# Regrouping a decoder layer's up projections, down passes and attention stages on one Trainium2 core

## The chip, the core and the metric

The kernel runs on one NeuronCore of a Trainium2 chip. Its engines are TensorE (PE in the profile; PEld is its weight load), VectorE (DVE), ScalarE (ACT), GpSimd (POOL) and SyncE (SP, which here only issues transfers). The metric is the device time of one execution in microseconds, as the median of several runs. A profiled execution additionally yields the span of the core and a trace of every instruction.

## The reference

One decoder layer in float32, for one sequence of 256 tokens and a width of 2048:

```python
h = rmsnorm(x, norm_mix_pre)
xr, yr, q, k, v, g_rnn, g_attn = split(h @ w_in)
y_rnn = rg_lru(causal_depthwise_conv(xr), ...) * gelu(yr)
y_att = sliding_window_sink_attention(rope(q), rope(k), v, sinks)   # 32 query, 4 key heads of 64
mix = sigmoid(g_rnn) * (y_rnn @ w_rnn_proj) + sigmoid(g_attn) * (y_att @ w_attn_proj)
x = x + rmsnorm(mix @ w_out, norm_mix_post)
h = rmsnorm(x, norm_mlp_pre)
u = square(relu(h @ w_mlp_up))                                       # 2048 -> 8192
x = x + rmsnorm(u @ w_mlp_down, norm_mlp_post)                       # 8192 -> 2048
```

The attention window is 128 tokens, worked in blocks of 128: the first block of queries (tb = 0) sees 128 keys, the second (tb = 1) sees 256. The scores are masked, the softmax has one more term per head (the sink), and the probabilities multiply the values.

## The kernel before

**Split products.** A float32 value is split into a high part (rounded to a format that TensorE multiplies at full rate) and a low part (the rest). A product is then high x high + high x low + low x high, three matmuls. Activations are split when they are made; weights are split as they stream in.

**The weight stream.** Class `Stream` (L54 to L156) loads weights as halves of 128 x 1024 float32 (512 KB) on SP's queue into four buffers `wraw` (L76), casts each to its high part `whi` on ScalarE (L94) and subtracts on VectorE for the low part `wlo` (L95). There are six buffers each of `whi` and `wlo`. `ws.half()` hands out the next half and calls `ahead`, which splits up to six halves beyond and loads up to ten beyond; `ws.half(False)` splits no more than it hands out. A buffer of `whi` or `wlo` is written again when TensorE has used it, a `wraw` when both parts are made.

**Two kinds of passes.** In `a_pair` (L243) the weights stand in TensorE's array and the activations stream through, so the result is transposed (channels in partitions). One `a_pair` computes 256 channels for 256 tokens. It takes four halves: f = 0 and 1 are two blocks of 128 channels, and each has two halves of the 2048 inputs. For a half, eight matmuls of 512 columns multiply the high weights with both parts of the activations (they stand side by side), and eight of 256 columns multiply the low weights with the high activations, into the second half of the same bank. At the end ScalarE copies one half of the result and VectorE adds the other (L260, L261). `a_pair` makes the inputs of the convolution and of the gelu (16 pairs), and 30 of the 32 pairs of the up projection; the first two have their own code (`up_pair`). In `b_step` and `b_pass512` the activations stand and the weights stream, always 512 columns wide.

**Work placed between.** A list `waiting` holds generators (`keys_values`, `attention`, `merge`, `residual`). Each call of `pump()` runs the first one to its next `yield`. A pass of the attention gates pumps eight times, a pass of queries four times, and an `a_pair` four times. So a `yield` moves the rest of a generator by one such step in program order. The order of instructions on each engine is then set by a planner before the run: it takes the instructions in program order as their priority, picks for each engine the first that is ready by its own estimate of costs, and gives out buffers as it goes. `pin` keeps instructions in the order written, `high_priority` moves them forward, and `issue_after` puts them behind a named instruction of their queue. On the chip each engine runs its instructions in that order and waits where an input is late.

**Attention.** For a group g of eight heads the stages are rope and transposes of the queries, then `scores` (products on PE, then scale, mask and maximum on VectorE, L543 and L545), `softmax` (maximum with the sink, exponentials on ScalarE at L559, division on VectorE at L564), `turn_probs` (transposes on PE, L581, and copies on ScalarE), and the product with the values (L607). Scores of both blocks were traced ahead of `softmax(0)`. The first norm's `first_norm` (L411) multiplies a diagonal with ones on PE (L425, tile `pr`) to spread the row scale over the partitions as `rT`; the convolution reads it.

**The MLP's beginning.** The second half of the rows of the out projection ends while the first half is already being multiplied with the up weights: `up_step` (L951), 48 products for tb = 0 with high weights, of which 26, 6, 6 and 6 stand ahead of the four transposes `turned(1, q)` of the second block (L958).

**The down projection.** It runs twice (f = 0, 1, each with 4096 of the 8192 inputs) over two passes n of 1024 output columns. The inputs are 16 pairs p of 128-row blocks. Seven of them (`SEVEN`: 0, 2, ... 12) are multiplied as 2 x 2 blocks with seven products instead of eight (`LEFT`): sums of weight blocks (`split_sums`, L114, tiles t, thi, tlo) with sums of activations (tile `seven`). The other nine are plain: two halves, four output blocks, three matmuls each. The last two (14, 15) are held, and done one output block after the other, so that `finish` can begin on the first while others still run. Output blocks lie in eight banks: P1, P6, Q5, N7 in two pairs of banks (tile `s`), which `a_pair` uses too, and P2, Q3, Q4, Cs in four single banks (tiles `dP`, `dQ`, `dCs`). When pair 12 is done, ScalarE and VectorE combine the seven products (L1102 to L1106), and `early` adds what the first half of the MLP had left in DRAM (`acc`). In the last pass two of these four additions ran on GpSimd, and `early` issued the two 1 MB loads of the residual `x1` on ScalarE's queue (L1174). `finish` adds, squares, normalises with the last gain, adds the residual (L1200) and stores.

**Room.** The pool `big` has 12 buffers of 8 KB a partition. uT (the plain pairs' activations) takes five, h2T four in the first half of the MLP, acc two in the second; t, thi and tlo take one each, later g3, `spare` and x1 as well.

## Time and profile before

| | |
|---|---|
| median of three runs | 1519.63 us (1518.05 to 1521.94) |
| profiled execution | 1518.56 us |
| its span | 1516.8 us |
| granted clock of TensorE | 0.997 |
| busy: PE, DVE, ACT, POOL | 99%, 73%, 55%, 0% |
| read from HBM | 288.60 MB, 194 GB/s over the span |

In the profile a row of the groups gives line, engine, operation, output <- inputs, shape and count, then busy time in us and the mean in ns. A row of the waits reads "engine, line <- who released it: us in total, times, longest". A row of the chain gives start, duration, engine, tile and line. A row of a timeline gives start, duration, engine, line, operation and tiles, and in brackets the idle time before it with its releaser. The duration of one matmul (0.39 us) contains its way through the array; the next one starts earlier, so spacing is read from starts. All starts are us from the start of the span.

### The profile page before, as it was taken

Reading aid. Unit: us, or ns where it says so; the run is one execution under the profiler, and the core shown is the slowest. Engines: PE = TensorE matmul, PEld = TensorE weight load, DVE = VectorE, ACT = ScalarE, POOL = GpSimd, SP = SyncE. Lnnn points to the kernel's source line nnn. Section 1 sums busy time; section 2 is a strip of 40 time slices with the busy share of each in tenths; the row PEclk is TensorE's granted clock in tenths of the full one; section 3 lists DMA queues with packets and bytes.
Section 4 is the critical chain, followed back from the end, with each engine's and each line's share of the span. In section 5 each row is a group of like instructions: output and inputs, shape, how many; then the busy total and the mean of one; then the engine's idle time right before and its main releaser. Section 6 shows DMA issues by size and latency. Waiting matters only on the chain.

```text
span 1516.8 us, 20055 instructions
## 1 busy us (share of the span) xinstructions
PE 1496.4 (99%) x7600; PEld 1259.9 (83%) x7600; DVE 1103.0 (73%) x1377; ACT 828.7 (55%) x1143; POOL 5.5 (0%) x11
## 2 busy tenths in 40 slices
PE   9999999999999999999999999999999999999997
PEld 7787778788888888888888888888888888888885
DVE  6666677858769967555657866688886666688897
ACT  6554654747566756443355655555454555555453
POOL 0000000000000000000000000000000000000001
PEclk9999999999999999999999999999999999999998
DMA  6645445455646565555764755566667565566564
GB/s 253 219 143 187 142 131 182 150 186 165 218 157 221 168 208 194 192 183 193 270 220 138 271 192 189 183 189 215 218 200 239 198 189 187 181 236 207 208 212 176
DMA packets 82896, 296.20 MB, mean 195 GB/s; under 512 B 9712, under 2 KB 9968, under 8 KB 81648
## 3 DMA queue, kind: packets, MB, share of 16 engines
q1 hardware_dynamic: 79056, 284.43, 57.3%
q10 hardware_dynamic: 3744, 10.50, 1.9%
q8 instruction: 59, 0.97, 0.3%
q14 instruction: 37, 0.30, 0.1%
HBM read 288.60 MB, written 6.29 MB: 194 GB/s over the span
## 4 chain that ended last, share of the span: by engine, by line
PE 82%; DVE 9%; DMA 5%; ACT 2%; issue 2%; DVEq 0%; SPq 0%; ACTq 0%
PE ps L253 22%; PE ps L256 11%; PE dQ L1061 4%; DMA wraw<-in_w_dn 4%; PE pp L271 4%; PE pp L275 4%; PE pp L273 4%; PE g L271 3%; PE g L275 3%; PE g L273 3%; DVE wlo L95 3%; PE s L1061 2%; PE dP L1061 2%; PE q L273 2%; PE q L275 2%; PE q L271 2%
## 5 line engine op out<-in xcount | busy, mean ns | idle before, releaser
L95 DVE TENSOR_TENSOR wlo<-wraw,whi 128x1024 fp32r<-128x1024 f32 x523 | 635.1, 1223 | 314.0 <-ACT whi L94 313.1
L94 ACT CAST whi<-wraw 128x1024 fp32r<-128x1024 f32 x523 | 544.5, 1052 | 576.6 <-PE ps L253 134.2
L253 PE MATMUL ps<-h2T,whi 128*128 128x512 f32 x960 | 240.5, 393 | 0.0
L253 PEld LDWEIGHTS ps<-h2T,whi 128*128 128x128 f32 x960 | 172.8, 189 | 30.8
L256 PEld LDWEIGHTS ps<-h2T,wlo 128*128 128x128 f32 x960 | 131.0, 191 | 9.3
L256 PE MATMUL ps<-h2T,wlo 128*128 128x256 f32 x960 | 133.9, 283 | 0.0
L253 PE MATMUL ps<-hT,whi 128*128 128x512 f32 x512 | 129.7, 394 | 0.0
L1061 PE MATMUL dQ<-whi,uT 128*128 128x512 f32 x288 | 106.9, 389 | 0.0
L253 PEld LDWEIGHTS ps<-hT,whi 128*128 128x128 f32 x512 | 91.9, 189 | 17.6 <-issue 1.5
L271 PE MATMUL g<-whi,hT 128*128 128x512 f32 x256 | 101.3, 396 | 0.0
L273 PE MATMUL g<-wlo,hT 128*128 128x512 f32 x256 | 100.1, 391 | 0.1
L275 PE MATMUL g<-whi,hT 128*128 128x512 f32 x256 | 99.9, 390 | 0.0
L256 PEld LDWEIGHTS ps<-hT,wlo 128*128 128x128 f32 x512 | 69.9, 190 | 5.0
L256 PE MATMUL ps<-hT,wlo 128*128 128x256 f32 x512 | 71.6, 283 | 0.0
L1061 PEld LDWEIGHTS dQ<-whi,uT 128*128 128x128 f32 x288 | 54.1, 188 | 11.2
L271 PEld LDWEIGHTS g<-whi,hT 128*128 128x128 f32 x256 | 48.1, 188 | 10.5 <-issue 1.0
L1061 PE MATMUL dQ<-wlo,uT 128*128 128x512 f32 x144 | 56.2, 390 | 0.5 <-DVE wlo L95 0.5
L275 PEld LDWEIGHTS g<-whi,hT 128*128 128x128 f32 x256 | 48.1, 188 | 10.1
L273 PEld LDWEIGHTS g<-wlo,hT 128*128 128x128 f32 x256 | 48.2, 188 | 10.0 <-DVE wlo L95 0.5
L1061 PE MATMUL dCs<-whi,uT 128*128 128x512 f32 x144 | 54.1, 389 | 0.0
L1061 PE MATMUL dP<-whi,uT 128*128 128x512 f32 x144 | 54.1, 389 | 0.0
L130 DVE TENSOR_TENSOR tlo<-t,thi 128x1536 fp32r<-128x1536 f32 x28 | 49.2, 1757 | 5.4 <-ACT thi L129 5.3
(280 smaller groups left out, 2464.8 us busy)
## 6 DMA issues: line engine op xcount, KB each, us to landing
wraw<-in_w_up SPq DMA_DIRECT2D x128, 512.0 KB, 4.8
wraw<-in_w_dn SPq DMA_DIRECT2D x128, 512.0 KB, 4.6
wraw<-in_w_g SPq DMA_DIRECT2D x64, 512.0 KB, 4.5
wraw<-in_w_xy SPq DMA_DIRECT2D x64, 512.0 KB, 4.6
wraw<-in_w_q SPq DMA_DIRECT2D x32, 512.0 KB, 4.5
wraw<-in_w_ap SPq DMA_DIRECT2D x32, 512.0 KB, 4.4
wraw<-in_w_rp SPq DMA_DIRECT2D x32, 512.0 KB, 4.3
wraw<-in_w_out SPq DMA_DIRECT2D x32, 512.0 KB, 5.2
```

What stands on the lines that cost most here:

```text
L94: self.pin(self.nc.scalar.copy(hi, src))
L95: self.pin(self.nc.vector.tensor_tensor(lo, src, hi.bitcast(F32), ALU.subtract))
L130: v.tensor_tensor(lo, t, hi.bitcast(F32), ALU.subtract)
L253: mm(both, hi[:, k * P : k * P + P], a.rearrange("p a b -> p (a b)"), start=half == 0 and k == 0, stop=False)
L256: mm(ps[:, f, 1, :], lo[:, k * P : k * P + P], a[:, 0, :], start=False, stop=half == 1 and k == 7)
L271: mm(banks[tb][n], a[:, 0, t], hi[:, n * 512 : n * 512 + 512], start=first, stop=False)
L273: mm(banks[tb][n], a[:, 0, t], lo[:, n * 512 : n * 512 + 512], start=False, stop=False)
L275: mm(banks[tb][n], a[:, 1, t], hi[:, n * 512 : n * 512 + 512], start=False, stop=last)
L1061: mm(b, a[x], w[y], start=not begun and i == 0, stop=tail and i == 2)
```

## The change

- `a_pair` takes its four halves in another order: the high products of halves 0 and 1 and the first one of half 2, then the low products of all four halves, then the other high products of half 2 and those of half 3. The number and widths of the products stay. The calls to `ws.ahead` stand behind the low products of halves 0 and 1 and ahead of the last high group.
- `first_norm` no longer multiplies on PE; `spread_out` does, behind the key transposes of the first block.
- `softmax(0)` is traced ahead of the scores of block 1, and two more `yield`s stand ahead of `turn_probs(0)`.
- 30 instead of 26 up products stand ahead of the first `turned(1, 0)`, and none is left behind the last.
- The passes n = 0 of the down projection run in the order 1, 0, 3, 2, 5, 4, 7, 6, 9, 8, 11, 10, 12, 13, 14, 15; the weight stream is reordered to match. The first (plain) pair runs output block by output block through `step`. The passes n = 1 keep their order.
- In the last pass all four additions of `early` run on VectorE, and the residual is loaded on SP's queue behind the last weight load (`residual_back`).

```diff
+TURNS = ((1, 0, 3, 2, 5, 4, 7, 6, 9, 8, 11, 10, 12, 13, 14, 15), tuple(range(PAIRS)))
...
-            self.nc.sync.dma_start(t, self.chunks[j // 2][:, c])
+            self.load = self.nc.sync.dma_start(t, self.chunks[j // 2][:, c]).ins
...
-            sums.update(len(chunks) + i for i in SEVEN)
-            chunks += [w_dn[(2 * f + n) * PAIRS + i] for i in range(PAIRS)]
+            sums.update(len(chunks) + i for i, p in enumerate(TURNS[n]) if p in SEVEN)
+            chunks += [w_dn[(2 * f + n) * PAIRS + p] for p in TURNS[n]]
...
-        for f in range(2):
-            both = ps[:, f].rearrange("p a b -> p (a b)")
-            for half in range(2):
-                hi, lo = ws.half()
-                act = [acts[kt // 4][:, kt % 4] for kt in range(half * 8, half * 8 + 8)]
-                for k, a in enumerate(act):
-                    mm(both, hi[:, k * P : k * P + P], a.rearrange("p a b -> p (a b)"),
-                       start=half == 0 and k == 0, stop=False)
-                for k, a in enumerate(act):
-                    mm(ps[:, f, 1, :], lo[:, k * P : k * P + P], a[:, 0, :], start=False,
-                       stop=half == 1 and k == 7)
-                pump()
+        def run(j, part, ks=range(8)):
+            f, half = j // 2, j % 2
+            for k in ks:
+                kt = half * 8 + k
+                a, w = acts[kt // 4][:, kt % 4], parts[j][part][:, k * P : k * P + P]
+                if part:
+                    mm(ps[:, f, 1, :], w, a[:, 0, :], start=False, stop=j == 1 and k == 7)
+                else:
+                    mm(ps[:, f].rearrange("p a b -> p (a b)"), w, a.rearrange("p a b -> p (a b)"), start=kt == 0,
+                       stop=j == 3 and k == 7)
+        at = ws.at
+        parts = [ws.half()]
+        run(0, 0)
+        parts.append(ws.half(False))
+        run(1, 0)
+        pump()
+        parts.append(ws.half(False))
+        run(2, 0, (0,))
+        run(0, 1)
+        ws.ahead(at + 1)
+        pump()
+        run(1, 1)
+        ws.ahead(at + 2)
+        run(2, 1)
+        parts.append(ws.half(False))
+        run(3, 1)
+        pump()
+        run(2, 0, range(1, 8))
+        ws.ahead(at + 3)
+        run(3, 0)
+        pump()
...
-            mm(pr[:, tb * P : tb * P + P], ones, dg, start=True, stop=True)
-        nc.scalar.copy(rT, pr[:, 0:S])
+    def spread_out():
+        pr = bank(psm, "pr")
+        for tb in range(TB):
+            mm(pr[:, tb * P : tb * P + P], ones, spread[:, tb * P : tb * P + P], start=True, stop=True)
+        nc.scalar.copy(rT, pr[:, 0:S])
...
+            if tb == 0:
+                spread_out()
             yield
...
         scores(0, 0, [bank(psm, "sc") for par in range(2)])
+        softmax(0)
         scores(1, 0, [bank(psb, "sc") for par in range(2)])
         if not last_group:
             scores(1, 1, two_banks("sc"))
-        softmax(0)
         yield
         if last_group:
             scores(1, 1, [bank(psb, "sc") for par in range(2)])
         softmax(1)
+        yield
+        yield
         yield
         turn_probs(0)
...
-    for q, n in enumerate((26, 6, 6, 6)):
+    for q, n in enumerate((30, 6, 6, 6)):
...
-        for p in range(PAIRS - held):
+        for p in turns[:PAIRS - held]:
...
+            elif p == turns[0]:
+
+                step(p, [ws.half() for i in range(2)], DOWN_ORDER)
...
         parts = [[ws.half(False) for i in range(2)] for p in range(held)]
+        split()
...
-                (nc.gpsimd if n and tb else nc.vector).tensor_tensor(t, t, acc[tb][:, c], ALU.add)
-            if n == 1:
-                for tb in range(TB):
-                    x1.append(flat(unit(f"x1{tb}", F32)))
-                    nc.scalar.dma_start(x1[tb], x1_away[tb])
+                nc.vector.tensor_tensor(t, t, acc[tb][:, c], ALU.add)
+
+        def residual_back():
+
+            for tb in range(TB):
+                x1.append(flat(unit(f"x1{tb}", F32)))
+                with tc.issue_after(ws.load):
+                    ws.load = nc.sync.dma_start(x1[tb], x1_away[tb]).ins
...
-        down(f, n, uT, 2, [(0, 0), (0, 1), (1, 0), (1, 1)], finish, early, between)
+        down(TURNS[n], uT, 2, [(0, 0), (0, 1), (1, 0), (1, 1)], finish, early, between, residual_back)
```

More of the change, by code (lines that the diff above doesn't have):

```diff
@@ L409, in layer @@
     rT = pa.tile([P, S], F32, name="rT")
+    spread = t2("spread")
     def first_norm():
-        pr = bank(psm, "pr")
-        spread = t2("spread")
         for tb in range(TB):
@@ L1067, in layer, with down @@
     PLACE = {(0, 0): "Q4", (0, 1): "Cs", (1, 0): "P2", (1, 1): "Q3"}
-    def down(f, n, uT, held, order, finish, early, between=lambda p: None):
+    DOWN_ORDER = ((1, 1), (1, 0), (0, 0), (0, 1))
+    def down(turns, uT, held, order, finish, early, between=lambda p: None, split=lambda: None):
         two = [pair(f"s{i}") for i in range(2)]
@@ L1150, in layer @@
                 full.clear()
-        order = [(1, 1), (1, 0), (0, 0), (0, 1)]
+        order = DOWN_ORDER
         if f == 0:
@@ L1158, in finish @@
                     nc.scalar.dma_start(acc_away[tb][:, c], t)
-                down(f, n, uT, 2, order, finish, lambda ready: None)
+                down(TURNS[n], uT, 2, order, finish, lambda ready: None)
             continue
@@ L1203, in layer @@
         n = 0
-        down(f, n, uT, 2, order, finish, early)
+        down(TURNS[n], uT, 2, order, finish, early)
         n = 1
```

3 lines of the change are left out of this document (1 added, 2 removed).

## The prediction

> **What bounds the kernel now.** I read the page first (busy shares), then the waits of PE, then the chain that ended last over the whole span, then the timeline of single engines around each wait.
>
> ```profile
> span 1516.8 us, 20055 instructions
> PE 1496.4 (99%) x7600; PEld 1259.9 (83%) x7600; DVE 1103.0 (73%) x1377; ACT 828.7 (55%) x1143; POOL 5.5 (0%) x11
> L253 PE MATMUL ps<-h2T,whi 128*128 128x512 f32 x960 | 240.5, 393 | 0.0
> L253 PE MATMUL ps<-hT,whi 128*128 128x512 f32 x512 | 129.7, 394 | 0.0
> PE pt L581 <- DVE s L564: 3.6, 3, 1.4
> PE pr L425 <- DVE spread L424: 0.9, 1, 0.9
> PE ptr L898 <- DVE h L892: 0.7, 1, 0.7
> PE s L1061 <- DVE u L261: 0.6, 2, 0.3
> PE dQ L1061 <- DVE wlo L95: 0.5, 1, 0.5
> ```
>
> The profiled execution took 1518.56 us, 1.76 us outside its span, and lies 1.07 us under the median of the three runs (1519.63). I sum against the execution and carry the difference to the median.
>
> The reader is to see that TensorE is the bound throughout. The last five rows are waits of PE (us in total, times, longest). Their total is about 6 us, and they are the only large ones. The change removes no matmul, so it can gain only at these waits, at the spacing of the matmuls, and at the end, where other engines finish after PE.
>
> **Part 1, the four halves of `a_pair`.** Before, each half ran eight matmuls 512 wide (high part) and then eight 256 wide (low part), so the width changed eight times in a pair. After, the order is wide, 32 narrow, wide, and the last wide group runs on into the next pair's first: two changes in a pair. The chain of waits gives what a change of width costs:
>
> ```profile
> 827.54 5.76 PE ps L998 x48
> 833.30 1.84 PE ps L995 x8
> 853.31 1.84 PE ps L253 x8
> ...
> 984.59 1.85 PE ps L253 x8
> ...
> 1067.77 2.72 PE dQ L1061 x12
> 1070.49 2.72 PE dP L1061 x12
> ```
>
> In long runs 48 narrow matmuls take 5.76 us (120.0 ns each), and 12 wide ones start 2.72 us before the next twelve (226.7 ns each). Eight wide ones behind narrow ones take 1.84 us, 0.027 more than 8 x 0.2267. From 853.31 to 984.59 lie 47 halves, 2.793 us each; by the rates of long runs a half would be 1.813 + 0.960 = 2.773. So one wide-narrow turn costs 0.020 us. A pair now takes 4 x 2.793 = 11.173 us; after, 32 x 0.2267 + 32 x 0.120 + 0.020 = 11.114. The wide matmuls of this kind are 960 + 512 = 1472, 32 to a pair: 46 pairs. Gain 46 x 0.059 = **2.7 us**. The wide matmuls at 833.30, behind 48 narrow ones, take the same 1.84 as behind eight, so the cost does not grow with the narrow run.
>
> [...]
>
> The other side of this part is the weight buffers. The high halves of the third and fourth quarter are held until about 9.3 and 11.1 us into a pair (7.4 and 10.2 before), and the calls that split ahead come later. A half that takes such a buffer is needed only in the pair after next, 11 us or more later, while its cast and subtraction take 1.05 + 1.22 us. The cover is 8 us; I cost it at nothing. Without that cover each pair would wait up to 2.3 us.
>
> **Part 2, `spread_out`.** The two transposing products of the first norm now come behind the first key transposes.
>
> ```profile
> 43.79 0.39 PE L275 MATMUL g<-whi,hT 128*128 128x512 f32 x1
> 45.10 0.49 PE L425 MATMUL pr<-spread,ones 128*128 128x128 f32 x2 [0.92 <-DVE spread L424]
> ```
>
> PE loses 1.31 - 0.23 = 1.08 us here. The keys' rope and transposes come later than `spread`, so nothing is waited for at the new place; what is left is about 0.1 us of restart. Gain **1.0 us** (0 to 1.1: rT is used only in the convolution, 200 us later).
>
> **Part 3, attention.** `softmax(0)` is traced before `scores(1)`, and the probabilities are turned two stages later.
>
> ```profile
> 151.75 1.28 DVE L543 SCALAR_TENSOR_TENSOR s<-sc,mask 128x512 f32<-128x512 f32 x2
> ...
> 156.51 0.16 DVE L552 TENSOR_TENSOR stat<-stat,sink 128x8 f32<-128x8 f32 x1
> ...
> 161.89 1.29 DVE L564 TENSOR_TENSOR s<-s,stat 128x512 f32<-128x512 f32 x2
> 160.91 0.39 PE L271 MATMUL q<-whi,hT 128*128 128x512 f32 x1
> 162.73 1.23 PE L581 MATMUL pt<-ident,s 128*128 128x128 f32 x8 [1.43 <-DVE s L564]
> ```
>
> PE comes to the transposes of block 0 just after 160.91 and stands 1.59 us beyond its 0.23. VectorE had spent 151.75 to 156.51 on the scores of block 1 before it began the softmax of block 0. With the order turned, that softmax begins up to 4.8 us earlier, its last product ends near 158, and the two extra stages keep PE from coming before the end of the gate pass. Three waits of 3.6 us and 0.16 us of restart each make 4.1. The cover is thinner in the last group, where `scores(1, 1)` waits for its banks and three small VectorE operations (0.2 us each) now stand ahead; between 0 and 4.4 I take **3.6**.
>
> **Part 4, 30 instead of 26 products before the first turn to the MLP.**
>
> ```profile
> 812.90 3.27 PE L954 MATMUL ps<-h2T,whi 128*128 128x256 f32 x26
> 816.91 0.66 PE L898 MATMUL ptr<-ident,h 128*128 128x128 f32 x4 [0.74 <-DVE h L892]
> ```
>
> Four more at 0.12 fill **0.5 us** of that wait; VectorE's normalised row stays late for the rest, and ScalarE and VectorE behind the later turns keep their pace. Bounds 0 and 0.7.
>
> **Part 5, a plain pair opens the passes n = 0.**
>
> ```profile
> 998.80 0.39 PE L1061 MATMUL dQ<-thi,seven 128*128 128x512 f32 x1
> 999.48 0.50 PE L1061 MATMUL s<-thi,seven 128*128 128x512 f32 x1 [0.29 <-DVE u L261]
> 999.82 0.40 PE L1061 MATMUL s<-tlo,seven 128*128 128x512 f32 x1
> ```
>
> The first seven-product pair needs the second `s` pair of banks 3.4 us into the pass, while VectorE still empties it of the last up product (L261). PE loses 0.45 + 0.11 us, in both such passes. The plain pair writes only the four `d` banks, long free, for 24 x 0.227 = 5.45 us. Gain **1.1 us**.
>
> The new order of pairs ends ... 11, 10, 12, 13: two seven-product pairs follow each other, where a plain pair stood between. In the first MLP half, 12 room buffers less 5 for uT and 4 for h2T leave 3, one set of t, thi and tlo. So the second pair's thi can start only when the first pair's products are done:
>
> ```profile
> 1051.94 1.49 ACT L129 CAST thi<-t 128x1536 fp32r<-128x1536 f32 x1 [0.71 <-PE s L1061]
> 1053.46 1.76 DVE L130 TENSOR_TENSOR tlo<-t,thi 128x1536 fp32r<-128x1536 f32 x1 [0.68 <-ACT thi L129]
> 1057.41 0.39 PE L1061 MATMUL s<-whi,seven 128*128 128x512 f32 x1
> 1060.36 0.39 PE L1061 MATMUL dQ<-tlo,seven 128*128 128x512 f32 x1
> ```
>
> Cast and subtraction end 3.28 us after the release. PE asks for tlo 1060.36 - 1057.41 = 2.95 us into a pair; today a plain pair's 5.45 us lie ahead of that. Cost 3.28 - 2.95 + 0.11 = **0.45 us**, once: the second half has two more buffers free (acc's 2 in place of h2T's 4). Bounds: 0, and 3.3 us in each of the two passes if other casts stand ahead of thi.
>
> **Part 6, the end.** The residual's two loads leave ACT's queue at the last seven-product pair and go on SP's behind the last weights; two additions leave POOL for VectorE.
>
> ```profile
> 1483.64 8.09 DMA wraw<-in_w_dn
> wraw<-in_w_dn SPq DMA_DIRECT2D x20, 512.0 KB, 4.5
> x<-x_away ACTq DMA_DIRECT2D x2, 1024.0 KB, 8.7
> 1497.04 0.50 PE L1061 MATMUL dQ<-wlo,uT 128*128 128x512 f32 x1 [0.54 <-DVE wlo L95]
> 1498.82 2.38 DVE L1170 TENSOR_TENSOR t<-t,acc 128x512 f32<-128x512 f32 x2
> 1501.12 0.68 DVE L1187 TENSOR_TENSOR acc<-dQ,t 128x512 f32<-128x512 f32 x1
> 1505.58 0.39 PE L1061 MATMUL dQ<-whi,uT 128*128 128x512 f32 x1
> 1507.89 0.68 DVE L1187 TENSOR_TENSOR acc<-dQ,t 128x512 f32<-128x512 f32 x1
> ```
>
> One of the last weights took 8.09 us to land against a median of 4.5, with 2 MB of residual in flight. Without it the last four come some 3.6 us earlier, and PE's wait of 0.54 (0.7 with its restart) goes. VectorE's additions, now 2.38 us for two, become four of 0.6 each: the same 2.4 us, but done before the first product ends. Then VectorE follows PE instead of trailing it: the last sum starts at 1507.89, some 2.1 us after the last matmul is through; PE done 0.7 earlier and VectorE half a microsecond behind gives about 1505.6. Gain **2.2 us**, between 0.7 (the wait alone) and 2.7. The residual, 2 loads of 8.7 us issued near 1486.5, lands by 1496 to 1504 and is first read near 1502: that cover is thin if the two follow each other at that rate. SP has only output stores queued behind them.
>
> **Sum.** 2.7 + 1.0 + 3.6 + 0.5 + 1.1 - 0.45 + 2.2 = 10.65 us. 1518.56 - 10.65 = 1507.9 for a profiled execution; carried to the median, 1519.63 - 10.65 = **1509.0**.
>
> **The rivals.**
> - *Turns of width are free* and the 0.027 belongs to something else at those places, such as the first use of a new weight half. Against it: in the passes of 512-wide products new halves begin too, and twelves stand at 2.72. The time is 1509.0 + 2.7 = 1511.7. [...]
> - *Attention's waits stay*: the planner moves PE's visits forward with the earlier softmax, and PE again comes before VectorE. For it: today's visits come as early as the planner's costs allow. Against it: the two added stages. 1509.0 + 3.6 = 1512.6.
> - *The residual comes late*: it lands at 1504 rather than before 1502, the output of the first block waits, and the gain at the end is gone: 1511.2.
> - *The two seven-product pairs collide*: 3.3 us exposed in each pass, 6.6 instead of 0.45: 1515.2.
> - *Slower: weights run late in `a_pair`.* Buffers come free in a burst at the end of a pair, and the split for the next wide group arrives after PE. Place: the first wide matmuls of a pair, 46 times. It decides from 10.65/46 = 0.23 us a pair; with 0.5 us it gives 1509.0 + 23 = 1532. Against it are the 8 us of cover counted above and VectorE's 73%.
>
> **How the numbers follow.** Forecast 0.50; free turns 0.12; attention 0.14; residual 0.10; collision 0.07; late weights 0.07. The range reaches from 1505.5 (all upper ends: 2.8 + 1.1 + 4.4 + 0.7 + 1.1 + 2.7 = 12.8, and about a microsecond for small waits that move) to 1516.5, over the collision. About 0.3% (4.6 us, so 1515.1) is what a measurement of this kernel can tell from no change. Faster by more: the first four cases, 0.86. Within 0.3%: the collision, 0.07. Slower: late weights, 0.07.
>
> **What would show it.** In the new profile: pieces of 32 narrow matmuls at 120 ns and pairs at 11.11 us; no wait of `pr`; `pt` waits under 0.5 us; a shorter `ptr` wait; none on L261 at the opening of a down pass, but one of `dQ` on tlo or thi in the first n = 0 pass; weights at the end landing in about 4.5 us and the last sum on VectorE about half a microsecond behind PE. The prediction is wrong if waits of PE on whi or wlo appear inside the pairs, or if `pt` keeps its 3.6 us.

## The result: no change

The changed kernel takes 1518.54 us (median of 12 runs, 1515.97 to 1521.69), the kernel before 1517.99 us (12 runs beside them, 1515.59 to 1521.94): a ratio of 1.0001 with a 95% interval of 0.9993 to 1.001. Forecast were 1509.0 us and a range of 1505.5 to 1516.5. The profiled execution took 1519.77 us, with a span 1.2 us longer than that of before.

The first lines of the page after, span and busy times:

```profile
span 1518.0 us, 20007 instructions
PE 1496.0 (99%) x7600; PEld 1262.0 (83%) x7600; DVE 1100.2 (72%) x1379; ACT 828.7 (55%) x1143; POOL 1.7 (0%) x9
```

TensorE is the bound as before. Its waits after (who waited, for whom: us in total, times, longest):

```profile
PE pt L610 <- ACT pT L612: 3.2, 2, 2.3
PE ptr L377 <- DMA x<-in_x: 2.1, 1, 2.1
PE pt L610 <- DVE s L593: 1.6, 1, 1.6
PE dQ L1092 <- DVE tlo L132: 1.4, 3, 0.8
...
PE dQ L1092 <- DVE wlo L97: 0.8, 1, 0.8
PE pk L530 <- DVE k L513: 0.6, 1, 0.6
PE dQ L1092 <- DVE acc L1227: 0.4, 1, 0.4
PE ptr L929 <- DVE h L923: 0.3, 1, 0.3
```

Against the list of before, `pr` (0.9) and the waits on L261 (0.6) are gone, `ptr <- h` is down from 0.7 to 0.3, and the waits of `pt` on VectorE's softmax are down from 3.6 to 1.6. New are `pk` (0.6), a wait of `pt` on ScalarE's copies pT (3.2), and 2.6 us of the down products for tlo, wlo and acc, where before had 0.5 on wlo. The chain of waits after shows the regrouped `a_pair`:

```profile
1180.50 7.28 PE ps L258 x32
1187.78 3.83 PE ps L256 x32
1191.62 7.28 PE ps L258 x32
```

A pair takes 7.28 + 3.83 = 11.11 us, from 1180.50 to 1191.62, as forecast (11.114).

The lengths of the stages, from the starts of their first products in each trace, say where the gain went; the columns e1 to e12 are the experiments below, by their numbers. "Attention" is from the first gate product to the first product of attention's projection; "first down" is the down stage of f = 0, "last down" that of f = 1 to the end of the span. "Last load" is how far into that last stage the residual's load is issued, which stands right behind the last weight's on SP (for the two kernels without it, the end of the last weight's issue).

| us | before | after | pair alone (e1) | natural order (e2) | alternating (e3) | old attention (e4) | e5 | e6 | end alone (e7) | swap (e8) | e9 | e10 | e11 | e12 |
|---|---|---|---|---|---|---|---|---|---|---|---|---|---|---|
| attention | 267.05 | 267.97 | 266.93 | 268.77 | 269.32 | 266.46 | 269.83 | 270.40 | 266.87 | 270.19 | 266.62 | 264.86 | 264.47 | 264.46 |
| first down | 165.17 | 166.23 | 164.56 | 164.56 | 167.90 | 166.29 | 164.56 | 164.56 | 165.71 | 164.56 | 164.56 | 164.56 | 164.56 | 164.56 |
| last load | 146.7 | 150.8 | 147.6 | 148.4 | 152.7 | 152.8 | 144.8 | 144.8 | 145.8 | 152.2 | 147.0 | 147.5 | 145.8 | 148.8 |
| last down | 177.26 | 178.62 | 178.27 | 176.63 | 181.57 | 180.99 | 174.06 | 173.89 | 174.15 | 180.32 | 175.19 | 175.31 | 174.03 | 176.75 |
| span | 1516.8 | 1518.0 | 1514.6 | 1513.9 | 1523.2 | 1519.1 | 1512.5 | 1512.8 | 1513.6 | 1519.3 | 1510.6 | 1508.9 | 1507.2 | 1510.1 |

From before to after, all that lies between attention and the last down stage, but for the first down stage (the `a_pair` stages above all), is 3.0 us shorter. Attention is 0.9 longer, the first down stage 1.1, the last 1.4, and the start 0.9, where in this execution the first loads of x came 0.2 us later and TensorE's granted clock was 0.50 behind them, from 8.64 to 12.05 us: together 1.2 us longer. Two places were forecast to gain and lost, attention and the order of pairs, and the experiments take these apart.

One trace is one execution, and the table shows how far the same code varies between them. With the old code of attention (before, 1, 4, 7, 9) it takes 266.46 to 267.05 us, with both edits (after, 2, 3, 8) 267.97 to 270.19. The last down stage has the same code in kernels 2, 5, 6, 9, 10 and 11 and takes 173.89 to 176.63 us.

### The profile page after: what moved, and what is told of

It reads as the page before. It is cut to its first block, busy times and chain, and to the rows that moved or that the text cites. A ratio compares the mean times of both kernels' runs of the same rounds, so it can differ in the third digit from the quotient of the medians.

```text
span 1518.0 us, 20007 instructions
## 1 busy us (share of the span) xinstructions
PE 1496.0 (99%) x7600; PEld 1262.0 (83%) x7600; DVE 1100.2 (72%) x1379; ACT 828.7 (55%) x1143; POOL 1.7 (0%) x9
## 4 chain that ended last, share of the span: by engine, by line
PE 75%; DVE 12%; DMA 6%; ACT 4%; issue 3%; DVEq 0%; ACTq 0%; SPq 0%
PE ps L258 21%; PE ps L256 11%; DMA wraw<-in_w_dn 5%; DVE wlo L97 4%; PE pp L300 4%; PE pp L296 4%; PE pp L298 4%; PE dQ L1092 3%; PE g L300 3%; PE g L296 3%; PE g L298 3%; ACT whi L96 2%; PE s L1092 2%; PE o L298 2%; PE o L296 2%
## 5 line engine op out<-in xcount | busy, mean ns | idle before, releaser
L258 PE MATMUL ps<-h2T,whi 128*128 128x512 f32 x960 | 223.9, 390 | 0.0
L258 PEld LDWEIGHTS ps<-h2T,whi 128*128 128x128 f32 x960 | 178.2, 188 | 35.6
L258 PE MATMUL ps<-hT,whi 128*128 128x512 f32 x512 | 121.2, 391 | 0.0
L256 PEld LDWEIGHTS ps<-h2T,wlo 128*128 128x128 f32 x960 | 119.1, 192 | 2.3
L256 PE MATMUL ps<-h2T,wlo 128*128 128x256 f32 x960 | 119.9, 283 | 0.0
L256 PEld LDWEIGHTS ps<-hT,wlo 128*128 128x128 f32 x512 | 63.7, 192 | 1.2
L256 PE MATMUL ps<-hT,wlo 128*128 128x256 f32 x512 | 64.7, 283 | 0.0
L300 PEld LDWEIGHTS g<-whi,hT 128*128 128x128 f32 x256 | 48.1, 188 | 10.2
L296 PE MATMUL q<-whi,hT 128*128 128x512 f32 x128 | 51.7, 404 | 0.0
```

The costliest lines, as they stand in the source:

```text
L256: mm(ps[:, f, 1, :], w, a[:, 0, :], start=False, stop=j == 1 and k == 7)
L258: mm(ps[:, f].rearrange("p a b -> p (a b)"), w, a.rearrange("p a b -> p (a b)"), start=kt == 0, stop=j == 3 and k == 7)
L296: mm(banks[tb][n], a[:, 0, t], hi[:, n * 512 : n * 512 + 512], start=first, stop=False)
L300: mm(banks[tb][n], a[:, 1, t], hi[:, n * 512 : n * 512 + 512], start=False, stop=last)
```

## The experiments

All ratios are to the kernel before, run beside them on the same chip, with 95% intervals. No kernel leaves work out; the last adds some.

**1. The new `a_pair` alone, on the kernel before.** The body of `a_pair` is that of the change, all else is as before.

> The kernel before with the new order of halves in a_pair alone. Theory: the pairs take 11.114 us as in the changed kernel (7.281 wide, 3.833 narrow), so 46 pairs save 2.7 us and the median lies 2.5 to 3 us under the kernel before; the waits of PE stay those of before (pt 3.6, pr 0.9, ptr 0.7, s 0.6, dQ 0.5 us). Rival: what the pairs save is given back by later weights (waits of PE on whi or wlo inside or behind the pairs), and the median stays within 0.5 us of before.

Measured: 1516.1 us, ratio 0.9978 (0.9963 to 0.9992). Waits of this kernel's PE:

```profile
PE pt L604 <- DVE s L587: 4.4, 3, 1.5
...
PE dQ L1084 <- DVE wlo L95: 1.1, 2, 0.8
PE pr L448 <- DVE spread L447: 0.9, 1, 0.9
PE ptr L921 <- DVE h L915: 0.7, 1, 0.7
```

The span is 2.2 us shorter, with 0.94 us saved in the 16 pairs of the last up stage (178.75 to 177.81), 0.059 a pair. And the whole list holds no wait on L261: the opening of the down passes is no longer late, and the first down stage takes 164.56 us without any new order of pairs. Which of the regrouped products brings that was not taken apart. The wait that Part 5 was to remove had been removed by Part 1.

**2. The change with the natural order of pairs in all passes.**

```diff
-TURNS = ((1, 0, 3, 2, 5, 4, 7, 6, 9, 8, 11, 10, 12, 13, 14, 15), tuple(range(PAIRS)))
+TURNS = (tuple(range(PAIRS)), tuple(range(PAIRS)))
```

> The changed kernel with both passes of the down projection in the natural order 0 to 15 (no plain pair first). Theory: the two seven-product pairs in a row (10, 12) make VectorE late at the end of pass n = 0, and PE pays for it in pass n = 1. So PE's waits on tlo, wlo and acc (about 1.0 us near 1101 to 1123 and 3.2 us from 1424 to 1469) go, the two waits on L261 (0.56 us each) come back, and the last weights and the last sum come 2 us earlier: 3.5 to 5 us under the changed kernel. Rival: the waits in the last pass come from the edits of the end (four additions on VectorE, residual on SP), and stay; then it is no faster than the changed kernel, or 1 us slower.

Measured: 1515.45 us, 0.9973 (0.9959 to 0.9987). The waits on L261 did not come back, as experiment 1 leads one to expect, and of those in the down stages one of 1.0 us on tlo is left. The first down stage is 1.7 us shorter than after, the last 2.0, and by the ratios the whole is 4 us shorter. So the new order of pairs cost several times the 0.65 us that it was to save.

**3. Strictly alternating pairs: a plain one between any two seven-product ones.**

```diff
-... 9, 8, 11, 10, 12, 13, 14, 15)
+... 9, 8, 11, 10, 13, 12, 14, 15)
```

> The changed kernel with pass n = 0 in the order 1, 0, 3, 2, ... 11, 10, 13, 12, 14, 15: a plain pair first, but a plain pair also between 10 and 12. Theory (two in a row): the waits in pass n = 1 go and those on L261 stay away; 4 to 6 us under the changed kernel, and 1 us under the natural order. Rival: it is not the two in a row but that every seven-product pair lies one place later in the pass, so that the combining of the seven products and the sums for the next pass crowd at its end; then PE's waits on tlo and wlo in pass n = 1 stay at 3 us or more, and here, where pair 12 is later still, grow.

Measured: 1524.25 us, 1.0038 (1.0022 to 1.0055), slower than before. Its waits in the down products:

```profile
PE dQ L1092 <- DVE wlo L97: 3.4, 2, 2.9
PE dQ L1092 <- DVE t L1194: 1.1, 2, 0.8
PE dQ L1092 <- DVE tlo L132: 0.7, 1, 0.7
```

Here no two seven-product pairs meet within a pass, yet the 2.9 us come in the last stage, 104 us into it; some 1.6 us more go behind them, where the products start 0.43 us apart from 1447.80 to 1450.79 us instead of 0.23 (see the end). So the rival expectation came true, and not the theory. By the loads the stream keeps pace through the first pass and falls behind at its end: the 29th load is issued 54.5 us into the stage (55.2 in kernel 9, in natural order), the 37th at 82.1 (76.6). At that turn pair 12 is now the last but the two held ones. VectorE's timeline there:

```profile
1413.60 1.22 DVE L125 TENSOR_TENSOR t<-wraw,wraw 128x1024 f32<-128x1024 f32 x1 [4.46 <-DMA wraw<-in_w_dn]
...
1422.49 1.20 DVE L97 TENSOR_TENSOR wlo<-wraw,whi 128x1024 fp32r<-128x1024 f32 x1
...
1434.68 1.23 DVE L97 TENSOR_TENSOR wlo<-wraw,whi 128x1024 fp32r<-128x1024 f32 x1 [0.52 <-ACT whi L96]
```

From 1413.60 to 1434.15 VectorE has no idle time. The sums for the next pass's pair 0 come first, then, from 1416.49 on, the additions that combine the seven products and add acc, and only at 1422.49 the next subtraction, on which the loads wait.

**4. The change with attention as before.** `softmax(0)` behind the scores of block 1, one stage ahead of the turning.

```diff
-        softmax(0)
         scores(1, 0, [bank(psb, "sc") for par in range(2)])
         if not last_group:
             scores(1, 1, two_banks("sc"))
+        softmax(0)
...
-        yield
-        yield
         yield
         turn_probs(0)
```

> The changed kernel with attention's stages as before (scores of both blocks ahead of the softmax, one yield). Theory: in the changed kernel ScalarE takes the 16 exponentials of a group ahead of the weight casts (no cast from 94.87 to 108.21), the weights run late, and the copies of the turned probabilities stand behind casts that wait for a DMA; so PE's waits at pt (2.4, 1.1, 0.3 and 1.8 us before a transposing product) turn into those of before (0.2, 1.6, 1.6, 1.0), the half clock after the longest is gone, and the stretch from the first gate product to the first product of the attention projection is 1 to 3 us shorter. Rival: the waits at pt come from PE's earlier arrival after the lost pr wait; then they stay at 5 us in total.

Measured: 1519.03 us, 1.0 (0.9989 to 1.0011). Attention takes 266.46 us, 1.5 less than after, so its edits cost 1.5 us there, and up to 3.7 us against the other traces with both edits. The total did not follow. In this profile, 1.9 us over the kernel's median, the last down stage took 2.4 us more: the last load was issued 152.8 us into it, 2.0 later than after. The medians of the two kernels do not show the gain in attention either, and why is not shown. With the changed order this stage was 178.6 and 181.0 us long.

**5 and 6. One attention edit at a time, with the natural order.** Experiment 5 puts `softmax(0)` behind the scores again and keeps the two more stages; experiment 6 keeps the early `softmax(0)` and drops the two stages.

> The kernel of e2_natural with softmax(0) again behind the scores of both blocks; the two extra stages ahead of turn_probs stay. Theory: softmax(0) ahead of the casts is what starves the weight stream in attention, and the extra stages alone bring PE to the transposes later than VectorE is done (1.6 us before). So the waits at pt (5.5 + 1.6 us in e2_natural) fall under 1.5 us in total, and the stretch from the first gate product to the first product of the attention projection is 3 to 5 us shorter than in e2_natural (268.8), some 2 us shorter than in e1_pair (266.9); the median is 3 us under e2_natural. Rival: it is the extra stages that crowd the turning of block 1 against the next pass's casts; then pt waits on ScalarE's copies stay at 3 us or more.

> The kernel of e2_natural with the two extra stages taken out; softmax(0) stays ahead of the scores of block 1. Theory (softmax ahead of the casts starves the weight stream): waits at pt of 4 us or more in total, among them a long one after the exponentials, and weights' casts waiting for DMA in the query passes, as in e2_natural; the stretch is 268 to 269 us. Rival (the extra stages do it): pt waits fall to 2 us or less and the stretch to 266 us or less.

Measured: 1516.9 us, 0.9983 (0.9972 to 0.9993), and 1516.8 us, 0.9987 (0.9975 to 1.0). Waits of 5:

```profile
PE pt L610 <- DVE s L593: 4.6, 3, 1.7
PE pt L610 <- ACT pT L612: 2.8, 3, 1.7
```

and of 6:

```profile
PE pt L610 <- DVE s L593: 6.8, 4, 1.9
```

Each alone is worse than neither: 269.83 and 270.40 us of attention, against 266.46 to 267.05 without both; the mean granted clock of the two profiled executions is 0.999 and 0.997. Neither theory's stretch came true. With the stages alone the old waits on VectorE stay and waits on the copies come on top. With the early softmax alone PE's visit moves forward with it, and PE waits 1.4 to 1.9 us, four times rather than three: here the rival "attention's waits stay" had the right mechanism, at more than its price. What both runs show besides is a last down stage of 174 us when the weights come early (last load at 144.8); both profiles lie over 2 us under their kernels' medians.

**7. The end alone, on the kernel before.** The residual on SP behind the last weight, all four additions on VectorE.

> The kernel before with the edits of the end alone (four additions on VectorE, residual on SP's queue behind the last weights). Theory: the last weights land in about 4.5 us instead of 8.1, PE's wait of 0.54 us on wlo before the last products goes, and the last sum on VectorE starts closer behind PE (2.3 us before): 1 to 2 us less in the last down pass (177.26 us before). Rival: VectorE is the limit of the last pass, the additions taken from GpSimd eat what the loads gain, and the last down pass is within 0.5 us of before.

Measured: 1516.54 us, 0.9986 (0.9976 to 0.9996); the last down stage is 3.1 us shorter. VectorE's additions in it:

```profile
1496.15 1.89 DVE L1171 TENSOR_TENSOR t<-t,acc 128x512 f32<-128x512 f32 x3
1497.96 0.68 DVE L1191 TENSOR_TENSOR acc<-dQ,t 128x512 f32<-128x512 f32 x1
```

Three additions take 1.89 us where two took 2.38, and the first sum of the held pairs starts at 1497.96 instead of 1501.12. From the last load's issue to the end it is 174.15 - 145.8 = 28.4 us, before 177.26 - 146.7 = 30.5: Part 6's 2.2 us. In the other traces it is 27.8 to 29.3 us with this edit and 30.6 in kernel 1 without. The other microsecond is the earlier last load, which lies within what the same code varies by.

**8. Only the first two pairs exchanged: 1, 0, 2, 3, ... 15 in n = 0.**

> The changed kernel with only the first two pairs of pass n = 0 exchanged (1, 0, 2, 3, ... 15): a plain pair opens the pass and two seven-product pairs follow each other, 0 and 2, but early in the pass; the last six pairs stand as before. Theory: what costs time in the changed kernel is that pair 10 comes one place later and leaves VectorE late where pair 12, the combining of the products and the next pass's first sums follow; so here the waits in pass n = 1 go and both down stages are those of e2_natural (164.6 and 176.6 us) within 0.7 us, the collision of 0 and 2 costing 0.5 us or less at its place. Rival: any two seven-product pairs in a row cost VectorE a lag that it does not win back in the pass; then waits of 1 us or more on tlo or wlo in pass n = 1 stay.

Measured: 1522.31 us, 1.0023 (1.0011 to 1.0034). The first down stage does not suffer: 164.56 us is all its products without a wait, 2 x (7 x 21 + 9 x 24) x 0.2267 = 164.6. The last takes 180.32, with these waits:

```profile
PE dP L1092 <- DVE acc L1227: 1.9, 1, 1.9
PE dQ L1092 <- DVE tlo L132: 1.1, 1, 1.1
PE dQ L1092 <- DVE wlo L97: 0.7, 2, 0.4
```

Pairs 0 and 2 follow each other at the opening of the stage, and the waits come 74 to 121 us into it, at the turn to n = 1 and behind it. So the rival held in the last stage and the theory in the first. In the trace the thirteenth load of the stage's weights is issued 5.5 us later than in kernel 9 (17.98 against 12.45 us into the stage), the sixteenth 1.8 later, every one from the seventeenth on 3.6 to 5.2 later, and the last but one 5.2 (150.66 against 145.51).

**9. The change without its two losing parts:** natural order, attention as before, and all else of the change.

> The changed kernel with the three parts undone that the runs so far speak against: natural order of pairs in all four passes, softmax(0) behind the scores of block 1 and one stage ahead of the turning. Kept: the new a_pair, spread_out, 30 products, the end. My theory (each part that paid keeps its gain when the others are gone; the lag of the weight stream came only from two seven-product pairs in a row): first gate product to attention's projection 266.5 us, first down stage 164.6, last down stage to the end 174.0 to 176.6, so a span of 1509.0 to 1511.6 us and a ratio of 0.995 to 0.997. Rival (the last down stage depends on the state in which the stream enters it, and attention's stages had changed that): last down stage 178 to 181 as in the kernel with only attention undone, span 1513 to 1516, ratio 0.998 to 0.9995.

Measured: 1513.11 us, 0.9959 (0.9944 to 0.9974), which is faster than before and, by these ratios, 0.4% faster than the change. The span is 6.2 us under before. The theory's numbers held: attention 266.62, first down stage 164.56, last 175.19. They do not show its "only": experiment 3 has a lag without two seven-product pairs in a row. The residual's issue, from SP's timeline:

```profile
1482.44 0.90 SPq L1212 DMA_DIRECT2D x<-x_away  x2
```

The stage began at 1335.41, so the residual's issue is 147.0 us into it. In the changed kernel it is 1490.15 - 1339.36 = 150.8, from PE's and SP's timelines:

```profile
1339.36 0.39 PE L1092 MATMUL dQ<-whi,uT 128*128 128x512 f32 x1
```

```profile
1490.15 0.90 SPq L1214 DMA_DIRECT2D x<-x_away  x2
```

**10. Kernel 9 with the probabilities turned later.** The query passes let attention in after every half, and three more stages stand ahead of the turning, but the softmax keeps its old place.

```diff
-        yield
+        for i in range(1 if last_group else 4):
+            yield
         turn_probs(0)
...
-        waiting.append(attention(g, b_pass512(hT, [...])))
+        waiting.append(attention(g, b_pass512(hT, [...], 1)))
```

> The kernel e9_best with the probabilities turned later: in the query passes the stages are pumped after every half, and three more stages stand ahead of turn_probs(0) in all groups but the last. It asks whether the waits of the transposes (1.59 us, twice, on VectorE) can be had by stages at all. If PE's visit only comes too early: both waits go, the stretch falls from 266.5 to 263.0 to 264.0, span 3 us under e9_best. Rival (the copies of the turned probabilities then meet the weight casts on ScalarE, as in the runs with the changed stages): waits on pT of 2 us or more come in their place and the stretch is 266 to 270, span equal or longer.

Measured: 1511.1 us, 0.9949 (0.9932 to 0.9965). Its waits in attention:

```profile
PE pt L610 <- DVE s L593: 1.6, 1, 1.6
PE pt L610 <- ACT pT L612: 1.2, 2, 0.6
```

Kernel 9 has 4.4 us in three waits on VectorE. Two of them are gone; two waits of 0.6 on the copies are the price, so attention gained 1.8 us rather than the 3 expected. What moved is PE's visit. In kernel 9 and in kernel 10 the transposes of the second group stand so in PE's timeline:

```profile
162.23 1.23 PE L610 MATMUL pt<-ident,s 128*128 128x128 f32 x8 [1.42 <-DVE s L593]
```

```profile
163.02 1.03 PE L610 MATMUL pt<-ident,s 128*128 128x128 f32 x8
```

PE comes to them at 160.81 in the one and, with query products to do until then, at 163.02 in the other.

**11. One more stage in the last group too.** `range(2 if last_group else 4)` in the line above.

> The kernel e10_later with one more stage ahead of turn_probs(0) in the last group of heads too (two instead of one). Theory (the transposes' last wait on VectorE, 1.6 us at 266.8, is only a visit that comes too early): the wait goes, the stretch from the first gate product to attention's projection falls from 264.9 to about 263.2 us, ratio about 0.994. Rival (the copies or the values' product then come late for the projection, which follows the last group closely): a wait of 1.5 us or more on pT or on yatt in its place, the stretch 264.5 to 267.

Measured: 1509.47 us, 0.9939 (0.9926 to 0.9951), the fastest kernel of the study. But neither theory held: the last wait is still there,

```profile
PE pt L610 <- DVE s L593: 1.5, 1, 1.5
```

and PE runs the same products ahead of it. The stretch of attention is 0.4 us shorter, by the wait of `pk` (0.6 instead of 1.0); kernel 12, which has kernel 10's attention, is as short, so the edit is not shown to do it. Most of the 1.7 us between the two profiles lies in the last down stage, whose code is the same and whose last load was issued 1.7 us earlier. What ties that to this edit is not shown; the intervals of 10 and 11 overlap.

**12. VectorE's work alone, added to kernel 10.** Behind pair 2 of the last down stage's first pass:

```diff
+        def hold(p):
+            if p == 2:
+                for tb in range(TB):
+                    nc.vector.tensor_tensor(acc[tb], acc[tb], acc[tb], ALU.max)
...
-        down(TURNS[n], uT, 2, order, finish, early)
+        down(TURNS[n], uT, 2, order, finish, early, hold)
```

> The kernel e10_later with two additions to VectorE's work in the last down stage: behind pair 2 of the pass n = 0 each acc tile (128 x 2048) is compared with itself for the larger, which leaves it as it is and takes VectorE some 2.4 us each, 4.9 us in all. It does by itself what the changed order of pairs is held to do. Theory (weights that come late in this stage stay late to the end, because VectorE's part of each weight sets when the next load may start): loads from the middle of the stage on are issued 3 to 5 us later than in e10_later, and the last down stage takes 178 to 181 us instead of 175.3. Rival (VectorE has some 15% of the stage free and catches up): loads are back in step by the turn to n = 1, and the stage takes 174 to 176.6 us.

Measured: 1515.44 us, 0.9978 (0.9967 to 0.9989), and 176.75 us in the last down stage, 1.4 more than kernel 10: between the two expectations. By the medians the added work costs 4.3 us (1515.44 against 1511.1 us, and the intervals do not overlap; against kernel 11, which ran beside it, 6.0); the profiled execution, of 1511.90 us, is among the fastest of the ten. VectorE's timeline in it shows where the work goes. In kernel 10 (the bracket is the idle time before an instruction, with its releaser):

```profile
1350.30 1.22 DVE L97 TENSOR_TENSOR wlo<-wraw,whi 128x1024 fp32r<-128x1024 f32 x1 [1.26 <-ACT whi L96]
1353.88 1.23 DVE L97 TENSOR_TENSOR wlo<-wraw,whi 128x1024 fp32r<-128x1024 f32 x1 [2.36 <-ACT whi L96]
...
1360.83 1.76 DVE L132 TENSOR_TENSOR tlo<-t,thi 128x1536 fp32r<-128x1536 f32 x1 [0.15 <-ACT thi L131]
```

and with the added work:

```profile
1345.17 2.29 DVE L1245 TENSOR_TENSOR acc<-acc 128x2048 f32<-128x2048 f32 x1 [1.01 <-DMA acc<-acc_away]
...
1351.92 2.29 DVE L1245 TENSOR_TENSOR acc<-acc 128x2048 f32<-128x2048 f32 x1
...
1361.90 1.76 DVE L132 TENSOR_TENSOR tlo<-t,thi 128x1536 fp32r<-128x1536 f32 x1 [0.15 <-ACT thi L131]
```

The two comparisons take 4.6 us, and the first waits 1.01 us for acc. Most of these 5.6 us went into idle time that stood right there (1.26 + 2.36). Counted from the stage's first product (1333.56 and 1333.37), the subtraction at 1360.83 ends up 1.26 us late. Behind it the loads are 0.4 to 1.9 us later than in kernel 10, the last but one 1.35 (147.31 instead of 145.96 us into the stage), and the end comes 1.4 late. So VectorE's idle time at the opening takes up most of the work, and the rest is not seen to be won back over the next 120 us. By itself this trace proves little: without any edit to this stage, kernels 10 and 11 differ by 1.7 us in the last load. The medians are the evidence that VectorE's time alone costs, and they lie within the 3 to 5 us of the theory.

## Why the prediction was wrong, part by part

**Part 1, `a_pair`: right.** 11.11 us a pair; the up stages gained 0.94 us for 16 pairs, as 16 x 0.059; in experiment 1 the stages of the other 30 pairs gained 1.6. In the kernel before, 0.020 us for each turn from wide to narrow and back explains the rows, and experiment 1 finds a pair shorter by the 0.059 us that follow. The rival "weights run late" did not happen: no trace has a wait on whi or wlo inside the pairs. What this part was not credited with is the end of the waits on L261, 0.6 us in the first down stage.

**Part 2, `spread_out`: 1.0 forecast, 0.2 to 0.4 found.** The wait of `pr` went. But "The keys' rope and transposes come later than `spread`, so nothing is waited for at the new place" overlooked that PE, no longer held at `pr`, comes to the key transposes themselves earlier: `pk` now waits 0.6 to 1.0 us. In kernels 4 and 9 it is the only edit left of those that touch attention: 266.46 and 266.62 us, against 266.87 to 267.05 in before, 1 and 7, which have none.

**Part 3, attention: 3.6 us gained forecast, 1.4 lost** (267.97 against 266.62 in kernel 9; up to 3.6 in the other traces with both edits). The failed step is "With the order turned, that softmax begins up to 4.8 us earlier, its last product ends near 158, and the two extra stages keep PE from coming before the end of the gate pass", and with it the sum that let nearly all of the 4.1 us go. The softmax does begin earlier: the exponentials start at 99.90 us rather than 104.51, and two of the three waits on VectorE go. But on ScalarE they thereby pass two weight casts that stood ahead of them. ScalarE's timeline after:

```profile
108.21 2.94 ACT L96 CAST whi<-wraw 128x1024 fp32r<-128x1024 f32 x3
...
119.27 1.05 ACT L96 CAST whi<-wraw 128x1024 fp32r<-128x1024 f32 x1 [1.78 <-DMA wraw<-in_w_q]
...
122.77 1.07 ACT L612 COPY pT<-pt 128x512 f32<-128x512 f32 x2
```

The cast before 108.21 is at 93.83; in the kernel before there are two more, at 99.22 and 101.94. The casts bunch up, the loads of the query weights behind them come late (2.24 and 1.78 us of idle time), and the copies of the turned probabilities stand behind those casts. PE's timeline:

```profile
120.74 0.40 PE L300 MATMUL q<-whi,hT 128*128 128x512 f32 x1
123.40 0.66 PE L610 MATMUL pt<-ident,s 128*128 128x128 f32 x4 [2.26 <-ACT pT L612]
...
124.87 0.63 PE L300 MATMUL q<-whi,hT 128*128 128x512 f32 x1
125.30 0.63 PE L296 MATMUL q<-whi,hT 128*128 128x512 f32 x1
```

I had counted the wait on VectorE and not what else the two engines run in that order. That the passed casts make this wait is read from the trace; experiments 5 and 6 show that neither edit pays alone, and 10 that two of the waits can be had by moving the visit and leaving the softmax.

**Part 4, 30 products: right.** The first up stage became 1.3 us shorter, 0.8 by its 14 pairs and some 0.5 by the wait at the turn (0.7 to 0.3); 0.5 was forecast.

**Part 5, the order of pairs: 0.65 us gained forecast, some 5 lost** (1.7 in the first down stage, 3.4 in the last, against kernel 9). Two steps failed. The gain of 1.1 had gone to Part 1 already. And the collision was priced by the release of one buffer, 0.45 us in one pass, where the cost is VectorE's time and the loads that wait for it. A seven-product pair takes 1.23 + 0.69 + 0.69 + 2 x 1.22 + 1.76 = 6.8 us of VectorE (sums, two subtractions, tlo) and 21 x 0.2267 = 4.8 of PE; a plain one 2.4 of VectorE and 5.4 of PE. Alternating they keep pace within a pass; two of the first kind in a row do not. In the changed kernel's last stage, where 10 and 12 meet:

```profile
1387.10 1.23 DVE L125 TENSOR_TENSOR t<-wraw,wraw 128x1024 f32<-128x1024 f32 x1 [0.65 <-DMA wraw<-in_w_dn]
...
1394.38 1.22 DVE L125 TENSOR_TENSOR t<-wraw,wraw 128x1024 f32<-128x1024 f32 x1
```

The sums of the second pair start 7.28 us after those of the first, with VectorE busy but for 0.7 us of it, and PE needs them after 4.8: 2.5 us late. At the meeting itself PE loses little, because weights are in hand: nothing here, 0.24 us in the first down stage. But the loads behind it are late. Against kernel 9 the 26th load of the stage is issued 0.1 us earlier, the 30th 3.6 us later, and those behind it stay 2.8 to 4.3 us late to the end. The loss shows in n = 1, as waits on tlo, wlo and acc. In the last stage no such delay was seen to be won back: not the 3.6 to 5.2 us of experiment 8, and kernels 5 and 6, early by 1.5 and 1.8 us at the 17th load, are 2.2 early at the last. In kernel 10 the sums of one seven-product pair start 10.03 us behind those of the one before, with a plain pair between, and PE takes 21 + 24 products of 0.2267 = 10.2 for the two: little margin.

```profile
1355.33 1.23 DVE L125 TENSOR_TENSOR t<-wraw,wraw 128x1024 f32<-128x1024 f32 x1 [0.22 <-DMA wraw<-in_w_dn]
...
1365.36 1.23 DVE L125 TENSOR_TENSOR t<-wraw,wraw 128x1024 f32<-128x1024 f32 x1 [0.50 <-DMA wraw<-in_w_dn]
```

VectorE's share of 72% did not show it: in the down stages it is higher (in kernel 9, 83% over 164 us of the first and 86% of the last), and VectorE waits inside this loop for ScalarE's cast and for the load that its own subtraction let start (9.9 and 10.0 us from 1339 to 1500 us in the changed kernel). Two in a row are not the whole of it either, since experiment 3 lost more by bringing pair 12 up against the turn. Why the first down stage bears pair 0 and 2 in a row without loss (experiment 8) is open, and so is the share that the room buffers have; a fifth buffer for raw weights, which might give the loop slack, was not tried.

**Part 6, the end: right, and hidden.** Experiment 7 finds 2.2 us between the last load and the end; there the wait of 0.54 on wlo is gone and the last sum starts 0.6 us behind the start of PE's last product, where it was 2.3 before. In the changed kernel the last load comes 4.1 us later (150.8 against 146.7), and 178.62 - 150.8 = 27.8 us follow instead of 30.5: the gain is there and Part 5's delay covers it. "The residual late" did not happen.

**The sum.** Against kernel 9 the changed kernel's span is 7.4 us longer: attention 1.4, first down stage 1.7, last 3.4, the start 1.0, where the changed kernel waits 2.1 us for x rather than 1.4 and has the granted clock of 0.50 behind it. Kernel 9's span is 6.2 us under before, where Parts 1, 2, 4, 6 and the waits on L261 were priced at 2.7 + 1.0 + 0.5 + 2.2 + 1.1 = 7.5. Two rivals of the prediction came true together, where I had given them chances as if only one could. "Attention's waits stay" was priced at the 3.6 us not gained and cost 1.4 more, with most of the waits on ScalarE's copies (3.2 of 4.8 us) rather than on VectorE; the collision cost some 5 us of the 6.6 priced, in the passes n = 1 for the most part. The list of waits that the prediction called the only large ones left out two at the start, 1.3 us for x and 1.1 for `ones`, which no part of the change was aimed at.

## What to carry to other kernels

Where a stage's weights pass through two engines before use, compare that work with TensorE's for each piece in its order, not as an average: a piece that needs 6.8 us of VectorE against 4.8 of TensorE has to stand beside one that pays it back, and a delay taken early can be paid at the end. Price an edit in the order of work by everything that the engines involved run at that place: moving the softmax moved the weight casts. And before two parts of a change are both credited with a wait, ask whether the first leaves it for the second.

## What the runs showed of the hardware

In the changed kernel TensorE's granted clock is 0.50 twice, for 3.41 us each time: from 8.64 to 12.05 us, just behind the wait of 2.1 us for x, and from 124.69 to 128.11 us (us of the stretch, its busy times by engine, granted clock, DMA share, GB/s):

```profile
124.80:128.00 3.20, 3.20 (x9) 2.48 (x8) 0.00 (x0) 0.55 (x1) 0.00 (x0) 0.50 0.78 214
...
131.00:134.00 3.00, 3.00 (x14) 1.00 (x13) 1.83 (x2) 1.87 (x3) 0.00 (x0) 1.00 0.50 169
```

The products start 0.43 us apart there, as the rows from 124.87 show, instead of 0.23: eight of them, 1.6 us lost behind a wait of 2.3, as much as Part 3 lost in all. Kernel 2 waited longer at the same place and kept its clock:

```profile
124.00:127.00 3.00, 3.00 (x17) 2.50 (x16) 0.00 (x0) 1.66 (x3) 0.00 (x0) 1.00 0.71 205
```

Its wait there was 2.9 us. In experiment 3 the wait of 2.9 us on wlo ends at 1445.93 us, and behind it the products from 1447.80 to 1450.79 us start 0.43 us apart:

```profile
1445.93 0.50 PE L1092 MATMUL dQ<-wlo,uT 128*128 128x512 f32 x1 [2.89 <-DVE wlo L97]
...
1447.80 0.63 PE L1092 MATMUL dP<-whi,uT 128*128 128x512 f32 x1
1448.23 0.63 PE L1092 MATMUL dQ<-whi,uT 128*128 128x512 f32 x1
```

Apart from these two stretches the clock is 1.00 in the changed kernel up to 1510 us. In the kernel before, where no single wait of TensorE is longer than 1.43 us, it is 1.00 up to 1509 us. So in these traces a wait of 2.3 and one of 2.9 us each cost some 1.6 us more behind them, and another of 2.9 us did not; what decides it is not shown.

Products of 512 columns with both operands in fp32r start 0.2267 us apart. The six products of a group with the values, in plain float32, stand in the kernel before as 12 rows (`po`, L607) from 117.51 to 120.23 us, 0.45 us a product, so the split format ran at twice the rate of plain float32 here.
